# Two experts' rows kept on chip, a diagonal in the first norm, and router logits turned round

## The chip, the cores and the metric

One core of a Trainium2 chip runs the whole kernel. The metric is the device time of one execution in microseconds (us), the median over runs. The engines are TensorE (PE in the profile, with its weight loads as PEld), VectorE (DVE), ScalarE (ACT), GpSimd (POOL) and SyncE (SP), which only issues transfers.

## The reference, cut to what matters

The reference runs four layers over 512 tokens (256 context, 256 latent) of width 1024. Layer i uses attention, Mamba-2, mLSTM or MLA as its mixer and then a hierarchical mixture of 16 experts, of which each token uses two:

```
hx = rmsnorm(xs, norm1_g[i]) * (1.0 + sc1x) + sh1x      # first norm
... mixer ...; xs = xs + g1x * yx
hx = rmsnorm(xs, norm2_g[i]) * (1.0 + sc2x) + sh2x
lg = hx @ w_rg + b_rg                                   # 4 group logits
le = (hx @ w_re + b_re).reshape(4, 4)                   # 16 expert logits
# top group, top two of its experts, softmax weights w
out = sum over e of w[e] * ((silu(hx @ w_gate[e]) * (hx @ w_up[e])) @ w_down[e])
xs = xs + g2x * out
```

The context stream is treated alike with its own shifts, scales and gates. The output is `rmsnorm(xs)` of the latent tokens.

## The kernel before, in words

The residual stream stays on chip as four tiles `X[t]` of 128 tokens by 1024. Instructions are traced in program order and then put into each engine's queue by a scheduler that simulates the engines with a cost model, so an edit can move neighbours that it doesn't touch; `issue_after` pins a block behind one instruction. Weights stream through a ring of on-chip slots (`w`, `wl`) issued from SP.

**First norm** (`norm1_tiles`, four token tiles per layer). ACT squares the tile with a row sum (L289), DVE makes the variance (L291), POOL the power (L293, `rstd`), ACT scales the tile by it into `xn` (L316), TensorE transposes `xn` in eight blocks (L321) into two PSUM tiles `tr`, and ACT (first half, L327) and DVE (second half, L329) evict with scale and shift into `hf`, which is split into `hhi` and `hlo`.

**Router** (`route`, four tiles in layers 0 to 2, two in layer 3). The tile is transposed in eight blocks (L478), ACT copies them into `hT` (L480), and eight fp32 products with `hT` as the loaded weights and the 68 padded router columns `wr` as the moving side make the logits, tokens on partitions, in the PSUM tile `pr` (L482). DVE scales and shifts them (L489). A later chain of small DVE and TensorE steps makes the lists of tokens by expert.

**Experts** (`experts`, layers 0 to 2). Expert e gathers its up to 128 rows from DRAM, multiplies by gate and up (`gate_up`), and one expert later by down (`down`). The scaled rows `y` (L795, L796) are written to a DRAM table `yd` (`keep`, L800) for experts 0 to 14, from POOL, the last one from ACT. Expert 15's rows stay on chip as a pair `yh`, `yl` (L831, L832), with a selector `selT` that maps its slots to tokens.

**Combine** (`combine`, run inside the next layer's first norm). Eight indirect gathers on POOL (L931, two per token tile in the order `go`, the second of a tile adding onto the first) fetch each token's two rows from `yd`; rows of expert 15 point at a row of zeros. For each tile and half, TensorE adds `selT` times `yh` and `yl` (L942, L943) and the gathered rows through an identity product (L946) in one PSUM tile, DVE multiplies by the gate (L947) and adds to `X[t]` (L952, in part POOL, L950). The first L942 of a tile is pinned behind the last expert's last product (`end`).

L248 is a POOL memset of the next layer's modulation step, L225 the product of that step (weights `cs` of 32 columns in four column groups).

Of the kernel before, what the change touches and what calls it, by code (L numbers as in the profile page):

```python
# [7 lines left out]
F32 = mybir.dt.float32  # L8
# [15 lines left out]
class Trunk:  # L24
# [8 lines left out]
    def setup(self):  # L33
# [32 lines left out]
        self.ge = mask(OP.is_ge, F32, "mge")  # L66
        self.le = mask(OP.is_le, F32, "mle")
        self.gtb = mask(OP.is_gt, BF, "mgtb")
        self.onesb = self.const.tile([128, 128], BF, name="onesb")
        nc.vector.memset(self.onesb, 1.0)  # L70
        self.onesf = self.const.tile([128, 128], F32, name="onesf")
# [232 lines left out]
    def norm1_tiles(self, pool, hpool):  # L304
        nc = self.nc
        self.hhi, self.hlo = ([hpool.tile([128, 4, 512], F32R, name=f"h{n}{q}") for q in range(2)] for n in ("hi", "lo"))
        norms, trs = [], [None] * self.o["tl"]
        for t in range(4):
            s = t // 2
            if self.pending:  # L310
                with self.tc.issue_after(norms[-self.o["lag"]].ins) if len(norms) >= self.o["lag"] else ExitStack():
                    self.pending[0](t, trs[-self.o["tl"]])
            xn = pool.tile([128, D], F32, name="xn", bufs=2)
            r = self.rstd(self.X[t], xn)
            norms.append(self.last_var)
            nc.scalar.activation(xn, self.X[t], AF.Copy, scale=r)  # L316
            for h in range(2):
                ps = self.tr()
                for j in range(4):
                    c = (4 * h + j) * 128  # L320
                    tr = nc.tensor.transpose(ps[:, j * 128:(j + 1) * 128], xn[:, c:c + 128], self.ident)  # L321
                hf = pool.tile([128, 4, 128], F32, name="hf", bufs=2)
                for j in range(4):
                    a, b = self.A1[:, s, 4 * h + j:4 * h + j + 1], self.B1[:, s, 4 * h + j:4 * h + j + 1]
                    src = ps[:, j * 128:(j + 1) * 128]
# [4 lines left out]
                hi, lo = self.hhi[h][:, :, t * 128:(t + 1) * 128], self.hlo[h][:, :, t * 128:(t + 1) * 128]  # L330
# [4 lines left out]
                (nc.gpsimd if h < self.o["n1p"] else nc.vector).tensor_sub(lo, hf, hi)  # L335
            trs.append(tr)

    def h(self, j, c0=0, c1=512):
# [75 lines left out]
    def shift_logits(self, i):  # L414

        nc = self.nc

        ps = self.P.tile([128, 512], F32, name="wm", bufs=1)
        for j in range(8):
            nc.tensor.matmul(ps[:32, 0:2], self.wr[:, j, :32], self.shift[:, :, j], start=(j == 0), stop=(j == 7))  # L420
        v = self.const.tile([32, 2], F32, name="bcol")
        nc.vector.tensor_copy(v, ps[:32, 0:2])

        self.bw = self.const.tile([128, 2, 20], F32, name="bw")
        for s in range(2):
            r = ps[:, 64 + 32 * s:96 + 32 * s]
            nc.tensor.matmul(r, v[:, s:s + 1].to_broadcast([32, 128]), self.ident[:32, :32], start=True, stop=True)
            nc.vector.tensor_add(self.bw[:, s], r[:, :20], self.rb[:, i, :])

    def route(self, pool, small, i, tiles, C, dense=False):  # L430
# [10 lines left out]
        lt = le.rearrange("p (t g) k -> p t (g k)", t=T)  # L441
        half = lambda v, h: v.rearrange("p (k h j) -> p h k j", h=2, j=4)[:, h]
        hT, h2s = [], []
        pr = self.core()
        for ti, t in enumerate(tiles):
            s = t // 2
            x = self.X[t]
# [27 lines left out]
            for h in range(2):  # L475
                ps = self.tr()
                for j in range(4):
                    nc.tensor.transpose(ps[:, j * 128:(j + 1) * 128], h2[:, 4 * h + j::8], self.ident)  # L478
                v = ps.rearrange("p (j k) -> p j k", j=4)
                nc.scalar.activation(hT[ti][:, 4 * h:4 * h + 4, :], v, AF.Copy)  # L480
            for j in range(8):
                nc.tensor.matmul(pr[:, ti * 68:(ti + 1) * 68], hT[ti][:, j, :], wr[:, j, :], start=(j == 0), stop=(j == 7))  # L482
            r = None if dense else rows()
            for v, c in ((G, slice(0, 4)), (lt, slice(4, 20))):
                pv = pr[:, ti * 68:ti * 68 + 20][:, c]
                if dense:
                    nc.vector.tensor_add(v[:, ti], pv, bias[:, c])
                else:
                    nc.vector.scalar_tensor_tensor(v[:, ti], pv, r, self.bw[:, s, c], op0=OP.mult, op1=OP.add)  # L489

        def ranks(v, m, nm):

# [47 lines left out]
            nc.vector.tensor_add(self.comb, a12[:, :, 0, :], a12[:, :, 1, :])  # L540
            return

        pp = self.core()
# [74 lines left out]
    def slots_of(self, S, a12, pk, ps, T, oh, weights, count):  # L618
# [7 lines left out]
        nc.vector.tensor_scalar(rw, rw, 128.0 * 15, None, op0=OP.min)  # L626
# [5 lines left out]
        self.last = self.const.tile([128, 4], F32, name="last")  # L632
        t2 = S("t2", [T, 2])
        nc.vector.scalar_tensor_tensor(t2, ps.rearrange("p (t k) -> p t k", k=2), 1.0, a12[:, :, :, 15], op0=OP.add, op1=OP.mult)
# [94 lines left out]
    def experts(self, pool, i, tiles, yd, release):  # L729
# [3 lines left out]
        for x in xgs:  # L733
            nc.gpsimd.memset(x, 0.0)

        nc.gpsimd.dma_start(yd[15 * self.C:, :], xgs[-1][0:1, :])

        def chunk(v):

# [59 lines left out]
        def keep(e, y, eng):  # L799
            return eng.dma_start(yd[e * 128:(e + 1) * 128, :], y)  # L800
# [16 lines left out]
        sel = xgs[0][:, :512].rearrange("p (t k) -> p t k", t=4)  # L817
        pt = self.tr()
        for t in range(4):
            nc.vector.tensor_scalar(sel[:, t], self.slot, self.last[:, t:t + 1], None, op0=OP.is_equal)  # L820
            nc.tensor.transpose(pt[:, t * 128:(t + 1) * 128], sel[:, t], self.ident)
        sT = po.tile([128, 4, 128], F32R, name="selT")
        nc.scalar.activation(sT, pt.rearrange("p (t k) -> p t k", t=4), AF.Copy)
        sw = self.sw[:, 15:16]
# [4 lines left out]
        yh, yl = (po.tile([128, 2, 512], F32R, name="y" + k) for k in "hl")  # L829
        for nb in range(2):  # L830
            nc.scalar.activation(yh[:, nb], py[nb], AF.Copy, scale=sw)  # L831
            nc.vector.scalar_tensor_tensor(yl[:, nb], py[nb], sw, yh[:, nb], op0=OP.mult, op1=OP.subtract)  # L832
        return po, sT, yh, yl

    def experts_select(self, pool, i, tiles):

# [77 lines left out]
            late = s, *now  # L914
        down(7, *late)

    def combine(self, pool, sT, yh, yl, yd, tiles):

        nc = self.nc
        g2 = self.mod_rows(pool, "g2", 2, 1)  # L920
# [15 lines left out]
        def add(t, after=None):  # L936
            x, y, c = self.X[t], ys[t], self.o["cadd"][t]
            for h in range(2):
                k = slice(512 * h, 512 * h + 512)
                ps = self.core() if h in self.o["cc"] else self.acc()  # L940
                with self.tc.issue_after((after or end).ins):
                    nc.tensor.matmul(ps, sT[:, t], yh[:, h], start=True, stop=False)  # L942
                nc.tensor.matmul(ps, sT[:, t], yl[:, h], start=False, stop=False)  # L943
# [1002 lines left out]
    def layers(self, dense=False):  # L1946
# [3 lines left out]
        for i in range(first, 4):  # L1950
# [3 lines left out]
            with self.pool("layer") as self.lay:  # L1954
# [23 lines left out]
                self.wr = route.tile([128, 8, 68], F32, name="wr")  # L1978
# [11 lines left out]
            else:  # L1990
                with self.pool("moe_ring") as L:
# [3 lines left out]
                    listing.close()  # L1995
                    with self.pool("moe_experts") as pool:
                        if i < 3:
                            yd = self.DR.tile([15 * C + 1, D], F32, name=f"yd{i}")
                            last = ExitStack()

                            def release():
# [65 lines left out]
```

## Time and profile before

| what | value |
|---|---|
| time of three runs (median, lowest to highest) | 2086.03 us, 2084.34 to 2087.01 us |
| profiled execution: time, span | 2090.72 us, 2088.8 us |
| mean granted TensorE clock | 0.955 |
| PE, DVE, ACT, POOL busy | 91%, 66%, 50%, 26% of the span |

The span runs from the first to the last instruction; the profiled execution's time holds 1.9 us around it. Matmuls are pipelined and their ends are modelled, so 91% busy is not 91% of what TensorE can do; a time between two starts says more than one duration. Where the chain of waits shows the engine idle is where an edit can give time.

### The profile page before, as it was taken

Reading aid. Unit: us, or ns where it says so; the run is one execution under the profiler, and the core shown is the slowest. Engines: PE = TensorE matmul, PEld = TensorE weight load, DVE = VectorE, ACT = ScalarE, POOL = GpSimd, SP = SyncE. Lnnn points to the kernel's source line nnn. Section 1 sums busy time; section 2 is a strip of 40 time slices with the busy share of each in tenths; the row PEclk is TensorE's granted clock in tenths of the full one; section 3 lists DMA queues with packets and bytes.
Section 4 is the critical chain, followed back from the end, with each engine's and each line's share of the span. In section 5 each row is a group of like instructions: output and inputs, shape, how many; then the busy total and the mean of one; then the engine's idle time right before and its main releaser. Section 6 shows DMA issues by size and latency. Waiting matters only on the chain. (4 is left out here: it accounts for less than half of the span.)

```text
span 2088.8 us, 30243 instructions
## 1 busy us (share of the span) xinstructions
PE 1899.8 (91%) x10820; PEld 1408.4 (67%) x10820; DVE 1387.5 (66%) x2715; ACT 1036.7 (50%) x2144; POOL 537.3 (26%) x528
## 2 busy tenths in 40 slices
PE   5989989997999999998799789997979988998996
PEld 2965677775777777777677467885867755657442
DVE  3668557885697787777788662239578866486443
ACT  4447526774664545432577442245447755454121
POOL 2012232113464646444221310004231122001000
PEclk9999999998999999999899889998989999999998
DMA  9444758976485456547698547543669966708792
GB/s 349 157 152 160 260 173 305 397 280 174 153 261 184 147 186 178 177 147 276 244 393 328 171 146 239 212 153 109 236 206 388 395 199 222 286 11 286 266 366 93
DMA packets 173344, 473.27 MB, mean 227 GB/s; under 512 B 27817, under 2 KB 75041, under 8 KB 152704
## 3 DMA queue, kind: packets, MB, share of 16 engines
q1 hardware_dynamic: 148912, 401.98, 53.7%
q0 software_dynamic: 23568, 67.43, 9.9%
q8 instruction: 88, 1.44, 0.3%
q10 hardware_dynamic: 704, 1.82, 0.2%
q14 instruction: 72, 0.59, 0.1%
HBM read 452.41 MB, written 31.34 MB: 232 GB/s over the span
## 5 line engine op out<-in xcount | busy, mean ns | idle before, releaser
L743 DVE TENSOR_TENSOR elo<-wl,ehi 128x1024 fp32r<-128x1024 f32 x156 | 187.0, 1220 | 23.7 <-ACT ehi L742 22.8
L742 ACT ACTIVATE ehi<-wl 128x1024 fp32r<-128x1024 f32 x156 | 161.3, 1055 | 56.3 <-PE acc L203 32.2
L225 PE MATMUL wm<-w,cs 128*32 128x512 f32 x768 | 125.6, 645 | 21.6 <-DMA w<-in_w_mod_dram 21.4
L748 POOL DMA_INDIRECT xg<-hd,gi x48 | 64.4, 1341 | 288.7 <-PE tr L761 229.6
L1275 POOL TENSOR_TENSOR wcl<-w,wch 128x512 fp32r<-128x512 f32 x76 | 115.0, 1525 | 71.1 <-ACT wch L1274 62.1
L201 PE MATMUL acc<-hhi,wch 128*128 128x512 f32 (+1 forms) x336 | 132.0, 393 | 0.5 <-ACT wch L1274 0.5
L203 PE MATMUL acc<-split_hi,hlo 128*128 128x256 f32 x464 | 131.3, 285 | 0.1
L201 PE MATMUL acc<-split_hi,hhi 128*128 128x256 f32 x464 | 131.2, 287 | 0.0
L202 PE MATMUL acc<-split_lo,hhi 128*128 128x256 f32 x464 | 130.7, 284 | 0.0
L203 PE MATMUL acc<-hhi,wcl 128*128 128x512 f32 (+1 forms) x336 | 129.7, 387 | 0.0
L202 PE MATMUL acc<-hlo,wch 128*128 128x512 f32 (+1 forms) x336 | 129.1, 384 | 0.0
L201 PE MATMUL acc<-ehi,xTh 128*128 128x512 f32 x288 | 124.3, 431 | 3.5 <-ACT xTh L764 3.5
L202 PE MATMUL acc<-elo,xTh 128*128 128x512 f32 x288 | 118.5, 411 | 2.5 <-DVE elo L743 2.5
L203 PE MATMUL acc<-ehi,xTl 128*128 128x512 f32 x288 | 116.4, 404 | 0.0
L743 DVE TENSOR_TENSOR elo<-w,ehi 128x1024 fp32r<-128x1024 f32 x84 | 100.9, 1219 | 13.3 <-ACT ehi L742 13.3
L742 ACT ACTIVATE ehi<-w 128x1024 fp32r<-128x1024 f32 x84 | 87.0, 1052 | 27.5 <-PE acc L203 15.9
L1353 ACT ACTIVATE A<-A,lnb 128x128 f32<-128x128 f32 x256 | 78.9, 390 | 39.9 <-POOL A L1348 39.9
L201 PEld LDWEIGHTS acc<-split_hi,hhi 128*128 128x128 f32 x464 | 88.0, 191 | 11.1 <-issue 5.2
L196 DVE TENSOR_TENSOR split_lo<-w,split_hi 128x1024 fp32r<-128x1024 f32 x33 | 40.2, 1224 | 78.5 <-ACT split_hi L195 78.3
L378 POOL TENSOR_TENSOR x<-x,restmp 128x256 f32<-128x256 f32 (+1 forms) x46 | 50.2, 1091 | 157.9 <-DVE restmp L374 143.7
L203 PEld LDWEIGHTS acc<-split_hi,hlo 128*128 128x128 f32 x464 | 88.6, 191 | 2.7 <-DVE hhi L334 1.7
L202 PEld LDWEIGHTS acc<-split_lo,hhi 128*128 128x128 f32 x464 | 88.6, 191 | 0.7 <-issue 0.7
(621 smaller groups left out, 5432.8 us busy)
## 6 DMA issues: line engine op xcount, KB each, us to landing
w<-in_w_mod_dram SPq DMA_DIRECT2D x96, 1024.0 KB
wl<-in_moe_w_down_dram SPq DMA_DIRECT2D x47, 1024.0 KB
wl<-in_moe_w_gate_dram SPq DMA_DIRECT2D x82, 512.0 KB
wl<-in_moe_w_up_dram SPq DMA_DIRECT2D x82, 512.0 KB
w<-in_moe_w_gate_dram SPq DMA_DIRECT2D x46, 512.0 KB
w<-in_moe_w_up_dram SPq DMA_DIRECT2D x46, 512.0 KB
yd<-y POOLq DMA_DIRECT2D x42, 512.0 KB, 6.8
w<-in_ssm_w_in_dram SPq DMA_DIRECT2D x40, 512.0 KB
```

Source lines behind the costliest of these rows:

```text
L196: self.nc.vector.tensor_sub(lo, w, hi)
L201: mm(ps, a[0], b[0], start=start, stop=False)
L202: mm(ps, a[0], b[1], start=False, stop=False)
L203: self.last_mm = mm(ps, a[1], b[0], start=False, stop=stop)
L225: nc.tensor.matmul(st["ps"][32 * g:32 * g + 32, :], self.cs[:, j, :], w[:, 512 * g:512 * g + 512], start=(j == 0), stop=(j == 7))
L378: (nc.vector if last else nc.gpsimd).tensor_add(x, x, tmp)
L742: nc.scalar.activation(hi, v, AF.Copy)
L743: nc.vector.tensor_sub(lo, v, hi)
L748: nc.gpsimd.indirect_dma_start(out=xgs[e % len(xgs)], out_offset=None, in_=self.hd, in_offset=bass.IndirectOffsetOnAxis(ap=self.gi[:, e:e ...
L1275: (eng or self.nc.gpsimd).tensor_sub(lo, v, hi)
L1353: nc.scalar.activation(M[d][:, h, c], M[d][:, h, c], AF.Exp, bias=self.lb[:, c, k:k + 1])
```

## The change

- **Experts.** The rows of expert 14 stay on chip as those of expert 15 do: `yd` holds 14 experts and the zero row, there are two selectors and two pairs `yh`, `yl`, and `combine` adds four products per tile and half before the gathered rows, where there were two. The last write to `yd` is expert 13's, issued from ACT.
- **First norm.** The scaled copy `xn` is gone. DVE makes `dg`, the identity with its rows scaled by `rstd`, and TensorE multiplies `X[t]` blocks (as weights) by `dg`, a plain fp32 product where there was a transpose. In layers 1 to 3 (where `pending` is set) ACT evicts six of a tile's eight blocks, where it evicted four.
- **Router.** `wr` has 32 columns and is now the loaded side; `hT` moves. Product j writes the 32 partitions of column group j mod 4, so four partial sums stand in `part`. ACT copies them into `gl`, and one product with `fold` (four stacked 32 by 32 identities) sums them and turns them back, into the PSUM tile `pp`, which is now taken at the start of `route`.

```diff
+        self.fold = self.const.tile([128, 32], F32, name="fold")
+        nc.vector.tensor_add(self.fold, iv[:, 0], iv[:, 1])
+        for g in (2, 3):
+            nc.vector.tensor_add(self.fold, self.fold, iv[:, g])
...
-            r = self.rstd(self.X[t], xn)
-            nc.scalar.activation(xn, self.X[t], AF.Copy, scale=r)
+            r = self.rstd(self.X[t], pool.tile([128, D], BF, name="sq", bufs=2))
+            dg = pool.tile([128, 128], F32, name="dg", bufs=2)
+            nc.vector.tensor_scalar(dg, self.ident, r, None, op0=OP.mult)
...
-                    tr = nc.tensor.transpose(ps[:, j * 128:(j + 1) * 128], xn[:, c:c + 128], self.ident)
+                    tr = nc.tensor.matmul(ps[:, j * 128:(j + 1) * 128], self.X[t][:, c:c + 128], dg, start=True, stop=True)
...
-                    if h == 0:
+                    if h == 0 or (self.pending and j < 2):
...
-        pr = self.core()
+        pr, pp = self.core(), self.core()
...
+            part = pr[:, ti * 128:(ti + 1) * 128]
             for j in range(8):
-                nc.tensor.matmul(pr[:, ti * 68:(ti + 1) * 68], hT[ti][:, j, :], wr[:, j, :], start=(j == 0), stop=(j == 7))
+                g = 32 * (j % 4)
+                nc.tensor.matmul(part[g:g + 32], wr[:, j, :], hT[ti][:, j, :], start=(j < 4), stop=(j > 3))
+            gl = small.tile([128, 128], F32, name="gl", bufs=2)
+            nc.scalar.activation(gl, part, AF.Copy)
+            pv = pp[:, 128 + ti * 32:160 + ti * 32]
+            nc.tensor.matmul(pv, gl, self.fold, start=True, stop=True)
...
+        keep(13, y, nc.scalar)
         po = release()
-        keep(13, y, nc.gpsimd)
-        y = rows(14, down(*late))
-        keep(14, y, nc.scalar)
-        py = down(*gate_up(15, x))
+        for u in range(2):
+            sel = xgs[u][:, :512].rearrange("p (t k) -> p t k", t=4)
+            ...
+            py = down(*(gate_up(15, x) if u else late))
+            yh, yl = (po.tile([128, 2, 512], F32R, name=f"y{k}{u}") for k in "hl")
...
+                    for u, (sT, yh, yl) in enumerate(kept):
+                        nc.tensor.matmul(ps, sT[:, t], yh[:, h], start=(u == 0), stop=False)
+                        nc.tensor.matmul(ps, sT[:, t], yl[:, h], start=False, stop=False)
```

The row limit of the gathers, the table's size and the slot table `last` (one more small DVE step) follow.

## Rows read from the trace of the kernel before

**Rows 1.** Instructions of L946: until what TensorE sat idle (us, times).

```profile
  DMA w<-yd,ri: 51.5, 13
```

**Rows 2.** Timeline, layer 0 to 1: start, length, engine, line [idle before <- releaser].

```profile
465.00 0.69 ACT L796 ACTIVATE y<-core,slotw 128x512 f32<-128x512 f32 x1 [0.28 <-PE core L203]
...
472.59 0.35 ACTq L800 DMA_DIRECT2D yd<-y  x1
...
474.19 0.52 POOL L248 MEMSET mod<- 64x512 f32 x1 [7.67 <-DVE elo L743]
...
476.23 1.09 POOL L931 DMA_INDIRECT w<-yd,ri  x1 [1.52 <-DMA yd<-y]
...
479.83 0.39 PE L203 MATMUL core<-ehi,actTl 128*128 128x512 f32 x1
...
481.66 0.62 PE L943 MATMUL acc<-yl,selT 128*128 128x512 f32 x2
...
490.07 2.08 PE L946 MATMUL acc<-w,ident 128*128 128x512 f32 x2 [7.10 <-DMA w<-yd,ri]
```

**Rows 3.** Timeline, layer 1 to 2.

```profile
1157.59 0.69 ACT L796 ACTIVATE y<-core,slotw 128x512 f32<-128x512 f32 x1 [0.27 <-PE core L203]
...
1168.69 1.09 POOL L931 DMA_INDIRECT w<-yd,ri  x1 [1.37 <-DMA yd<-y]
...
1174.00 0.40 PE L203 MATMUL core<-ehi,actTl 128*128 128x512 f32 x1
...
1182.30 2.08 PE L946 MATMUL acc<-w,ident 128*128 128x512 f32 x2 [5.15 <-DMA w<-yd,ri]
```

**Rows 4.** Timeline, layer 2 to 3.

```profile
1694.44 0.69 ACT L796 ACTIVATE y<-core,slotw 128x512 f32<-128x512 f32 x1 [0.27 <-PE core L203]
...
1705.45 1.09 POOL L931 DMA_INDIRECT w<-yd,ri  x1 [7.54 <-DMA yd<-y]
...
1709.28 0.39 PE L203 MATMUL core<-ehi,actTl 128*128 128x512 f32 x1
...
1719.38 2.08 PE L946 MATMUL acc<-w,ident 128*128 128x512 f32 x2 [6.96 <-DMA w<-yd,ri]
...
1729.67 2.07 PE L946 MATMUL acc<-w,ident 128*128 128x512 f32 x2 [2.65 <-DMA w<-yd,ri]
```

**Rows 5.** Stretches: length, PE, PEld, DVE, ACT, POOL busy, clock, DMA, GB/s.

```profile
483.00:490.00 7.00, 0.00 (x0) 0.00 (x0) 1.13 (x2) 0.02 (x1) 5.37 (x4) 0.80 1.04 231
490.00:495.00 5.00, 4.93 (x7) 2.18 (x8) 1.76 (x3) 0.00 (x0) 0.00 (x0) 0.59 1.06 210
...
505.00:511.00 6.00, 3.12 (x16) 2.54 (x15) 4.73 (x14) 6.00 (x12) 1.48 (x2) 0.50 1.04 311
```

**Rows 6.** The experts' own gathers (min/median/max ns), instructions of L748.

```profile
L748 POOL DMA_INDIRECT xg<-hd,gi x48: 984/1412/1902, 308.7 to 1647.9; - x48
```

**Rows 7.** Groups by line and shape: busy us, mean ns.

```profile
L743 DVE TENSOR_TENSOR elo<-wl,ehi 128x1024 fp32r<-128x1024 f32 x156 | 187.0, 1220 | 23.7 <-ACT ehi L742 22.8
...
L316 ACT ACTIVATE xn<-x,rstd 128x1024 f32<-128x1024 f32 x16 | 18.3, 1150 | 11.5 <-POOL rstd L293 11.5
```

**Rows 8.** Timeline, first norm of layer 1 and Mamba-2 core: runs of like instructions.

```profile
511.48 1.50 ACT L327 ACTIVATE hf<-tr,B,A 128x128 f32<-128x128 f32 x4
...
515.66 1.03 PE L321 MATMUL tr<-ident,xn 128*128 128x128 f32 x8
...
605.24 0.83 PE L1376 MATMUL tr<-CT,st 128*128 128x128 f32 x6
```

**Rows 9.** Timeline, routers of layers 0 and 3, and one modulation step.

```profile
40.72 1.07 PE L225 MATMUL wm<-w,cs 128*32 128x512 f32 x8
...
289.32 0.67 PE L420 MATMUL wm<-shift,wr 128*32 128x2 f32 x16
...
297.72 1.90 PE L482 MATMUL core<-wr,h2T 128*128 128x68 f32 x16
...
1924.44 3.66 PE L482 MATMUL core<-wr,h2T 128*128 128x68 f32 x16 [2.70 <-DVE le L489]
```

More of the change, by code (lines that the diff above doesn't have):

```diff
@@ L68, in setup @@
         self.gtb = mask(OP.is_gt, BF, "mgtb")
+        self.fold = self.const.tile([128, 32], F32, name="fold")
+        iv = self.ident.rearrange("p (g c) -> p g c", g=4)
+        nc.vector.tensor_add(self.fold, iv[:, 0], iv[:, 1])
+        for g in (2, 3):
+            nc.vector.tensor_add(self.fold, self.fold, iv[:, g])
         self.onesb = self.const.tile([128, 128], BF, name="onesb")
@@ L312, in norm1_tiles @@
                     self.pending[0](t, trs[-self.o["tl"]])
-            xn = pool.tile([128, D], F32, name="xn", bufs=2)
-            r = self.rstd(self.X[t], xn)
+            r = self.rstd(self.X[t], pool.tile([128, D], BF, name="sq", bufs=2))
             norms.append(self.last_var)
-            nc.scalar.activation(xn, self.X[t], AF.Copy, scale=r)
+            dg = pool.tile([128, 128], F32, name="dg", bufs=2)
+            nc.vector.tensor_scalar(dg, self.ident, r, None, op0=OP.mult)
+            tok = slice(t * 128, (t + 1) * 128)
             for h in range(2):
@@ L329, in norm1_tiles @@
                         nc.vector.tensor_scalar(hf[:, j, :], src, a, b, op0=OP.mult, op1=OP.add)
-                hi, lo = self.hhi[h][:, :, t * 128:(t + 1) * 128], self.hlo[h][:, :, t * 128:(t + 1) * 128]
+                hi, lo = self.hhi[h][:, :, tok], self.hlo[h][:, :, tok]
                 if h:
@@ L334, in norm1_tiles @@
                     nc.vector.tensor_copy(hi, hf)
-                (nc.gpsimd if h < self.o["n1p"] else nc.vector).tensor_sub(lo, hf, hi)
+                nc.vector.tensor_sub(lo, hf, hi)
             trs.append(tr)
@@ L419, in shift_logits @@
         for j in range(8):
-            nc.tensor.matmul(ps[:32, 0:2], self.wr[:, j, :32], self.shift[:, :, j], start=(j == 0), stop=(j == 7))
+            nc.tensor.matmul(ps[:32, 0:2], self.wr[:, j, :], self.shift[:, :, j], start=(j == 0), stop=(j == 7))
         v = self.const.tile([32, 2], F32, name="bcol")
@@ L625, in slots_of @@
         nc.vector.tensor_add(rw, rw, ps)
-        nc.vector.tensor_scalar(rw, rw, 128.0 * 15, None, op0=OP.min)
+        nc.vector.tensor_scalar(rw, rw, 128.0 * 14, None, op0=OP.min)
         self.ri = self.const.tile([128, 8], I32, name="ri")[:, :T * 2]
@@ L630, in slots_of @@
         count()
-        self.last = self.const.tile([128, 4], F32, name="last")
-        t2 = S("t2", [T, 2])
-        nc.vector.scalar_tensor_tensor(t2, ps.rearrange("p (t k) -> p t k", k=2), 1.0, a12[:, :, :, 15], op0=OP.add, op1=OP.mult)
+        self.last = self.const.tile([128, 2, 4], F32, name="last")
+        t2 = S("t2", [2, T, 2])
+        for u in range(2):
+            nc.vector.scalar_tensor_tensor(t2[:, u], ps.rearrange("p (t k) -> p t k", k=2), 1.0, a12[:, :, :, 14 + u],
+                                           op0=OP.add, op1=OP.mult)
         nc.vector.tensor_reduce(self.last, t2, axis=AX.X, op=OP.add)
@@ L734, in experts @@
             nc.gpsimd.memset(x, 0.0)
-        nc.gpsimd.dma_start(yd[15 * self.C:, :], xgs[-1][0:1, :])
+        nc.gpsimd.dma_start(yd[14 * self.C:, :], xgs[-1][0:1, :])
         def chunk(v):
@@ L814, in experts @@
             x, late = nx, now
+        keep(13, y, nc.scalar)
         po = release()
[L817 to L824, printed above, removed]
-        keep(13, y, nc.gpsimd)
-        y = rows(14, down(*late))
-        keep(14, y, nc.scalar)
-        py = down(*gate_up(15, x))
[L829 to L833, printed above, removed]
+        kept = []
+        for u in range(2):
+            sel = xgs[u][:, :512].rearrange("p (t k) -> p t k", t=4)
+            pt = self.tr()
+            for t in range(4):
+                nc.vector.tensor_scalar(sel[:, t], self.slot, self.last[:, u, t:t + 1], None, op0=OP.is_equal)
+                nc.tensor.transpose(pt[:, t * 128:(t + 1) * 128], sel[:, t], self.ident)
+            sT = po.tile([128, 4, 128], F32R, name=f"selT{u}")
+            nc.scalar.activation(sT, pt.rearrange("p (t k) -> p t k", t=4), AF.Copy)
+            py = down(*(gate_up(15, x) if u else late))
+            sw = self.sw[:, 14 + u:15 + u]
+            yh, yl = (po.tile([128, 2, 512], F32R, name=f"y{k}{u}") for k in "hl")
+            for nb in range(2):
+                nc.scalar.activation(yh[:, nb], py[nb], AF.Copy, scale=sw)
+                nc.vector.scalar_tensor_tensor(yl[:, nb], py[nb], sw, yh[:, nb], op0=OP.mult, op1=OP.subtract)
+            kept.append((sT, yh, yl))
+        return po, kept
     def experts_select(self, pool, i, tiles):
@@ L915, in experts_select, with combine @@
         down(7, *late)
-    def combine(self, pool, sT, yh, yl, yd, tiles):
+    def combine(self, pool, kept, yd, tiles):
         nc = self.nc
@@ L1977, in layers @@
                 self.A2 = self.mod_rows(route, "A2", 2, 0)
-                self.wr = route.tile([128, 8, 68], F32, name="wr")
+                self.wr = route.tile([128, 8, 32], F32, name="wr")
                 self.router_weights(self.wr, i)
@@ L1997, in layers @@
                         if i < 3:
-                            yd = self.DR.tile([15 * C + 1, D], F32, name=f"yd{i}")
+                            yd = self.DR.tile([14 * C + 1, D], F32, name=f"yd{i}")
                             last = ExitStack()
```

8 lines of the change are left out of this document (2 added, 6 removed).

## Prediction

> **What bounds the kernel now.** I read the page first: TensorE is busy nearly everywhere, so time can come only from stretches in which it stands idle or runs at its lower clock. The view of one line's waits then tells where: before the identity products of the combine TensorE sat idle 51.5 us in all until gathered rows landed [rows 1] (a wait of the weight load and of its product are counted apart, so the wall time is about half of that). The timeline of the three layer changes shows how it comes about. In the first, expert 14's write to `yd` is issued at 472.59, the first gather can start at 476.23, when that write has landed, and the first product on gathered rows at 490.07, after 7.10 us of idle TensorE [rows 2]. The second and third look alike, with 5.15 and 6.96 us, and the third waits 2.65 us more on a later tile [rows 3, 4]. The view of stretches adds the clock: 0.80 granted in the idle stretch, 0.59 in the 5 us behind it, 0.50 in the norm [rows 5]. So the end is set there by write, gather, product, and then by a chain through DVE and ACT, not by TensorE's work.
>
> **The change, part by part.** The sum is made against the profiled execution, 2090.72 us; the median of three runs is 2086.03, 0.22% less, and the forecast is scaled to it.
>
> *A. The gathers start earlier.* Expert 14's write is gone; the last one is expert 13's. Its rows are ready at 465.00 + 0.69 = 465.69 [rows 2]. From issue on ACT to the first gather took 476.23 - 472.59 = 3.64 us [rows 2]; I take the same, so the first gather goes at 469.3, 6.9 us earlier. The write moves from POOL's queue to ACT's; there it holds the next weight conversion by about the 0.35 us that the issue took [rows 2], while the same issue for expert 14 falls away. The gathers keep their place in POOL's queue, and SP's next weight loads, which wait for the two ring slots that the gathered rows hold, move up with the additions that free them. From first gather to first product took 490.07 - 476.23 = 13.84 us [rows 2], so the rows are there at 483.2. Then TensorE itself is later: its last expert product starts at 479.83, and before the gathered rows come the selector products of the five pairs of tile and half for which PSUM has room, now 20 passes instead of 10, at 0.62 - 0.39 = 0.23 us each [rows 2]: 479.83 + 0.23 + 20 x 0.23 = 484.7. So the first identity product starts at 484.7, not 490.07: -5.4. In the second change 1158.28 + 3.64 + 13.84 = 1175.8 against 1174.00 + 21 x 0.23 = 1178.8, so -3.5 [rows 3]; in the third 1712.6 against 1709.28 + 4.83 = 1714.1, so -5.3 [rows 4]. Together -14.2. What is late next is TensorE, then DVE's gate products and additions, on which the other six selector passes hide (1.4 us a change, +4.1 in all if that cover is gone). Bounds: nothing if the gather is held by something else, -20.7 if the extra passes are covered too.
>
> Gathers now run under expert 15's weight splits on DVE, of 1.22 us each [rows 7], where they ran under little. The nearest rows are the experts' own gathers, which run under such splits: 1.41 us in the median, 0.98 at the least [rows 6], so 0.4 us more for each of the four gathers ahead of the first tile, 1.6 us; in the first change that makes 484.8 against TensorE's 484.7, and nothing in the sum. The Trainium skill, page "SBUF — State Buffer", section "Who interferes with whom", says that a DVE instruction with two SBUF inputs and a GpSimd instruction that reads SBUF shut each other out for a whole instruction; were each gather held by one whole split, the time would be that of the third rival, and the trace so far shows a third of that.
>
> *B. No cold start behind the wait.* In the 5 us behind the idle stretch the clock was 0.59 [rows 5]; without the stretch the same work takes 5 x 0.59 = 2.95 us at the full level, -2.0 for each of three changes, and the third saves its later 2.65 as well [rows 4], since its gathers are through before the modulation weights' loads set in. -8.7; bounds 0 (the clock stays low, DVE sets the pace) and -14 (the norm behind it warm too).
>
> *C. First norm.* Out of each tile's chain goes the scaled copy, 1.15 us [rows 7]. In comes `dg`, which no row shows: between nothing and one 128 by 128 eviction, 1.50 / 4 = 0.375 us [rows 8]; an eighth of a split of 1024 elements would be 0.15 [rows 7], so I take 0.25. A transposed block costs one pass; eight take 1.03 us. The plain fp32 product of the same shape in Mamba-2 is recorded as two passes, and six of those take 0.83, so a pass costs (1.03 - 0.83) / 2 = 0.10 in either form [rows 8]. Four blocks ahead of the first eviction then cost 0.40 more at the full level. Net -0.50 a tile; ACT's load per tile falls by 1.15 - 2 x 0.375 = 0.40, which bounds what a stage in which ACT is busy 6.00 of 6.00 us [rows 5] can give: about -1.5 in each of layers 1 to 3, -0.5 in layer 0, where the norm waits for modulation weights. -5.0. Bounds: at the half level, with all eight extra passes on the path, -1.15 + 0.25 + 8 x 0.20 = +0.7 a tile, +11; or the whole copy gained, -14.
>
> *D. Router.* The 16 passes of a tile's logits take 1.90 us [rows 9]. Turned round they load 32 columns and write four column groups. Bounds: 1.90 if nothing overlaps, and 0.67, which 16 passes with 32 loaded columns and two moving ones take [rows 9]. Nearest is the modulation product, eight passes of 512 columns in four groups in 1.07 us [rows 9], four times as much streaming a pass, so I take 0.8. New are the copy `gl` on ACT (0.375 as above) and two passes of `fold` (0.20): in the last tile they eat the gain; in the three tiles ahead 0.90 each is left, of which DVE's and ACT's own steps leave half: -1.3 in each of layers 0 to 2. In layer 3 the second tile's logits waited 2.70 us for DVE to read the first's out of the same PSUM tile [rows 9]; ACT now empties it: -2. Sum -5.9. The added wait is `fold`'s for ACT; behind it on TensorE stand the next tile's transposes. If they stand there each time, 14 tiles x 0.6 = +8.4; at best -14.
>
> *E. Small change.* Four more selector transposes per layer, 4 x 0.11, lie in the TensorE-bound expert loop: +1.3. Expert 14's split rows take DVE and ACT one step more than its plain rows; they lie under TensorE's products of expert 15. The zero-row write, `last` and `fold`'s set-up lie beside the lists and the first weight loads.
>
> Sum: -14.2 - 8.7 - 5.0 - 5.9 + 1.3 = -32.5: 2058.2 for the profiled execution, 2086.03 x (1 - 32.5 / 2090.72) = 2053.6 for the median.
>
> **The rivals.**
> 1. *The memset stays in front.* L248 waited on POOL until 474.19 for the experts' space and took 0.52 [rows 2]. If the scheduler leaves it ahead of the gathers, they start at 474.7 in the first change, 1.5 us earlier, and I take the same for the second; the third keeps its -5.3. A becomes -8.3, B loses 4.0: -22.6, 2063.5. For it: it stood there. Against: it came in while the gathers waited.
> 2. *The gain is eaten by the new TensorE waits.* C and D at their bad bounds: -14.2 - 8.7 + 11 + 8.4 + 1.3 = -2.2, 2083.8, no change. For it: 0.50 in the norm [rows 5]. Against: the clock fell behind idle TensorE, and the norm will have twice the passes; the transposes ahead of `fold` belong to other tiles.
> 3. *Gathers starve under the splits.* Each of the four gathers held by one split, 4.9 us: 488.1, 1180.7 and 1717.5, A = -2.0 - 1.6 - 1.9 = -5.5, and B's idle is back by half, -4.4: -19.5, 2066.6.
> 4. *Slower: the plain products cost four passes.* If a block against `dg` took four passes of 0.20, at the half level and on the norm's path, a tile would pay 8 x (0.80 - 0.20) = 4.8 less the 0.9 that copy and `dg` differ by, 16 tiles +62 in C's place: +34.5, 2120.5. It decides from 27.5 / 16 = 1.7 us a tile. Against it: two passes, each of 0.10 at the full level [rows 8]. The Trainium skill, "TensorE: Matmul & The Clock Gate", section "Terms", calls the transpose mode four times faster for fp32; row L1376 shows twice.
>
> **How the numbers follow.** Forecast 0.60; rival 1 0.18; rival 3 0.08; rival 2 0.08; rival 4 0.04; 0.02 for other ways of being slower. The range takes the forecast's own spread (B at -13, C and D doubled: about 2038) up to rival 1 with C and D at nothing (2074.4): 2038 to 2075. About 0.2%, 4 us, is what a measurement of this kernel can tell from no change; faster (the forecast, rivals 1 and 3) 0.86, same (rival 2) 0.08, slower 0.06.
>
> **What would show it.** In the changed trace the first gather goes 3 to 4 us after expert 13's rows, ahead of L248; L946's wait for gathered rows falls from 51.5 to under 10; the clock behind the last expert stays near 1.00. In the norm a tile has 16 passes at 0.10 and no L316. The 16 logit passes of a tile take under 1 us, and the fold stands clear of ACT's long steps. Wrong it would be if the gathers start no earlier than L248 ends, if the norm runs at 0.50 with TensorE waited for, or if TensorE idles ahead of `fold` in each tile.

## The result and the profile after

The changed kernel takes 2064.12 us (median of four runs) against 2086.52 us of the kernel before: ratio 0.9884, 95% interval 0.9869 to 0.9898. The forecast was 2053.6 us in a range of 2038 to 2075. The profiled execution went from 2090.72 to 2062.44 us, by 28.3 us. Of this, 22.4 us is the medians' difference; the profiled execution of before lay 4.2 us above its median and that of after 1.7 us below. So stretches read from the two traces sum to some 6 us too much. The two medians alone give a ratio of 0.9893; where variants are compared below by their ratios, each is taken against the kernel before in its own round, and the medians can give a difference that is up to 4 us another.

First, what TensorE waited for ahead of the identity products (L963 of the changed kernel). The row answers to [rows 1], where it stood at 51.5 us:

```profile
  DMA w<-yd,ri: 5.8, 6
```

The timeline of the first layer change answers to [rows 2]:

```profile
466.59 0.69 ACT L811 ACTIVATE y<-core,slotw 128x512 f32<-128x512 f32 x1 [0.33 <-PE core L209]
...
467.31 0.35 ACTq L815 DMA_DIRECT2D yd<-y  x1
...
470.38 1.23 DVE L758 TENSOR_TENSOR elo<-wl,ehi 128x1024 fp32r<-128x1024 f32 x1 [0.56 <-ACT ehi L757]
...
470.97 1.59 POOL L947 DMA_INDIRECT w<-yd,ri  x1 [9.49 <-DMA yd<-y]
...
472.67 2.36 DVE L758 TENSOR_TENSOR elo<-wl,ehi 128x1024 fp32r<-128x1024 f32 x2 [1.06 <-ACT ehi L757]
...
472.86 1.93 POOL L947 DMA_INDIRECT w<-yd,ri  x1 [0.30 <-issue]
...
475.10 1.00 POOL L947 DMA_INDIRECT w<-yd,ri  x1 [0.30 <-issue]
...
477.41 0.54 POOL L254 MEMSET mod<- 64x512 f32 x1
...
483.07 0.40 PE L209 MATMUL core<-ehi,actTl 128*128 128x512 f32 x1
...
487.84 1.02 PE L963 MATMUL acc<-w,ident 128*128 128x512 f32 x2
...
488.71 1.02 PE L963 MATMUL core<-w,ident 128*128 128x512 f32 x2
```

The first gather goes 470.97 - 467.28 = 3.69 us after expert 13's rows are ready, the memset stands behind four gathers, and the first identity product follows the last expert product after 4.77 us of selector products, without a wait and at the full level (1.02 us for two, 2.08 before). It is 2.2 us earlier than before, not 5.4: expert 13's rows are 1.6 us later than before, and the last expert product another 1.6 us.

The other two changes can be read from expert 13's rows to the first identity product, before [rows 3, 4] and after:

```profile
1145.02 0.69 ACT L811 ACTIVATE y<-core,slotw 128x512 f32<-128x512 f32 x1 [0.33 <-PE core L209]
...
1164.38 1.13 PE L963 MATMUL acc<-w,ident 128*128 128x512 f32 x2 [1.76 <-DMA w<-yd,ri]
...
1675.11 0.69 ACT L811 ACTIVATE y<-core,slotw 128x512 f32<-128x512 f32 x1 [0.33 <-PE core L209]
...
1696.43 1.02 PE L963 MATMUL acc<-w,ident 128*128 128x512 f32 x2
```

That way takes 20.56, 18.67 and 20.63 us where it took 24.38, 24.02 and 24.25: -3.8, -5.3 and -3.6, together -12.8 us. In the second change TensorE still waits 1.76 us for rows.

The view of stretches, to be held against [rows 5] (clock 0.59 behind the idle stretch, 0.50 in the norm):

```profile
487.80:492.80 5.00, 5.00 (x14) 2.27 (x13) 3.69 (x5) 1.05 (x2) 0.40 (x1) 1.00 1.01 200
502.70:508.70 6.00, 5.91 (x37) 5.94 (x38) 3.15 (x9) 4.37 (x12) 0.55 (x1) 0.72 1.10 378
```

In the second change the whole norm is warm as well. Its 17 us, of before (from L321's first row on, at 1193), then of after (from L329's, at 1177):

```profile
1193.00:1210.00 17.00, 6.24 (x33) 4.56 (x32) 15.62 (x35) 15.54 (x32) 1.55 (x3) 0.62 0.32 111
```

```profile
1177.00:1194.00 17.00, 14.47 (x116) 12.48 (x115) 12.67 (x34) 12.88 (x31) 2.73 (x7) 1.00 0.63 219
```

The norm and the router by line, over the whole run (busy us, mean ns). Of before: L321 21.0 us in 128 passes, L482 30.6 us in 224.

```profile
L329 PE MATMUL tr<-dg,x 128*128 128x128 f32 x256 | 36.1, 292 | 5.1 <-ACT hf L335 3.0 <-DVE var L297 1.7 <-DVE hf L337 0.3
...
L493 PE MATMUL core<-h2T,wr 128*32 128x128 f32 x224 | 11.5, 293 | 1.6 <-ACT h2T L489 1.3
L497 PE MATMUL core<-fold,gl 128*128 128x32 f32 x28 | 5.6, 283 | 4.9 <-ACT gl L495 4.4 <-DVE le L503 0.5
```

TensorE has 15.1 us more to do in the norm and 13.5 us less in the router. Steps of their timelines, against [rows 8, 9]:

```profile
297.62 0.64 PE L493 MATMUL core<-h2T,wr 128*32 128x128 f32 x16
...
298.33 0.28 ACT L495 ACTIVATE gl<-core 128x128 f32<-128x128 f32 x1
...
299.64 0.41 PE L497 MATMUL core<-fold,gl 128*128 128x32 f32 x2
...
497.60 1.95 PE L329 MATMUL tr<-dg,x 128*128 128x128 f32 x16
...
497.94 0.28 DVE L323 TENSOR_SCALAR dg<-ident,rstd 128x128 f32<-128x128 f32 x1
```

**A ledger by stretch.** Like instructions that occur equally often in two traces are matched in order; the median difference of their starts is how far the later kernel is ahead at that place, and a row is how much that changed over a stretch (us, negative is gained, each against the profiled execution of before). "Change 0 to 1" reaches from expert 13's rows to about 60 us behind the combine. The columns other than the first are experiments of the next section. The profiled executions lie off their medians by different amounts: in the order of the columns -1.7, 0.0, 0.0, 2.3, 1.1, 6.0 and 5.6 us, so that a difference between two columns is off by as much.

```
stretch                    whole  experts  norm  router  no norm  no router  late write
layer 0 up to its router     3.2     1.0    2.8     1.4      0.5        3.3         2.8
router 0                    -2.3     0.0    0.0    -2.3     -2.3        0.0        -2.3
change 0 to 1               -6.1    -6.4   -3.4     1.3     -5.4       -7.5        -1.8
rest of Mamba-2, router 1   -8.6     0.7    3.3    -9.7     -2.1       -2.2        -7.4
change 1 to 2              -10.3   -10.6    0.7     1.6    -11.3      -10.0        -5.3
rest of mLSTM                4.4     2.3    3.9     0.4     -1.9        7.7         3.9
router 2                    -1.5     0.6    0.3    -2.0     -2.2       -0.1        -2.0
change 2 to 3               -6.9    -8.4    1.7     0.9     -3.9       -2.9         1.3
rest of MLA                  1.3     7.4    1.0     7.1      0.1        0.5         0.7
router 3                    -2.0     0.1    0.3    -2.0     -2.0       -0.1        -2.0
lists, experts, last layer   1.3     1.1   -0.8    -1.1      1.1        1.2         1.7
sum                        -27.5   -12.3    9.9    -4.4    -29.4      -10.1       -10.4
```

In the whole, the layer changes give 23.3 us, near the 22.9 of A and B; the norms of layers 1 to 3, for which C had 4.5 more, lie in the same rows. But mixers that the change doesn't touch move by up to 9 us either way, and layer 0 loses 3.2. The experiments ask what each part is worth and where these come from.

### The profile page after: what moved, and what is told of

It is laid out like the page before. It is cut to its first block, busy times and chain, and to the rows that moved or that the text cites. A ratio compares the mean times of both kernels' runs of the same rounds, so it can differ in the third digit from the quotient of the medians.

```text
span 2060.3 us, 30756 instructions
## 1 busy us (share of the span) xinstructions
PE 1899.6 (92%) x11036; PEld 1411.8 (69%) x11036; DVE 1394.9 (68%) x2728; ACT 1036.1 (50%) x2172; POOL 536.4 (26%) x525
```

## The experiments

**The three parts alone**, each the lines of the change that belong to it. Of the experts' part:

```diff
+        keep(13, y, nc.scalar)
...
+        for u in range(2):
...
+                    for u, (sT, yh, yl) in enumerate(kept):
```

> The kernel before with the experts' part of the change alone (rows of experts 14 and 15 on chip; first norm and router as before). By the sum it carries A, B and E: -14.2 - 8.7 + 1.3 = -21.6 us, a ratio of 0.9897. The trace of the changed kernel gives for the same part -7.0, -2.0 and -11.7 at the three layer changes and +1.4 in lists and experts: -19.3, 0.9908. Rival: the earlier gathers pay only with the new norm, because behind the combine the old norm's chain through ACT would be late next; then about half, -10 us, 0.995.

Measured: 2077.27 us, ratio 0.9962 (0.9947 to 0.9977). At the three layer changes the trace gives 25.4 us, so the rival falls there, though its number (0.995, half the gain for want of the new norm) is near: 7.4 us go again in MLA, which no expectation had.

```diff
-            nc.scalar.activation(xn, self.X[t], AF.Copy, scale=r)
...
+            nc.vector.tensor_scalar(dg, self.ident, r, None, op0=OP.mult)
```

> The kernel before with the first norm's part alone. By the sum C = -5.0 us, ratio 0.9976. From the changed kernel's trace (+3.2 in layer 0's norm and mixer, -7.1, -2.5 and +4.5 in the three others) -1.9 us, 0.9991, with layer 0 later by some 3 us. Rival: the bad bound of C, all extra passes at the half clock on the path, +11 us, 1.0053.

Measured: 2100.27 us, ratio 1.0075 (1.0057 to 1.0093). The number is beyond the rival's, but its mechanism is not what the trace shows: where the new norms stand, the ledger has +2.8 in layer 0 and -3.4, +0.7 and +1.7 at the three changes, together +1.8. The rest is in mixers and in an odd place, the unchanged router of layer 1. Its timeline and stretch in this kernel (L484 is the router's product):

```profile
976.25 0.40 PE L429 MATMUL wm<-ident,bcol 32*128 32x32 f32 x2 [3.25 <-DVE var L291]
...
983.55 3.52 PE L484 MATMUL core<-wr,h2T 128*128 128x68 f32 x16
...
992.64 3.65 PE L484 MATMUL core<-wr,h2T 128*128 128x68 f32 x16 [0.55 <-DVE le L491]
```

```profile
980.00:990.00 10.00, 10.00 (x49) 9.60 (x48) 5.78 (x12) 2.98 (x5) 3.67 (x5) 0.50 0.98 386
990.00:998.00 8.00, 5.75 (x26) 5.41 (x26) 2.03 (x10) 0.00 (x0) 0.00 (x0) 0.50 0.18 71
```

The router ran at the lower level, 3.5 us for what takes 1.90 [rows 9], and the kernel fell back by 7.7 us between the end of Mamba-2 and the lists. Of this, 5.0 are in the products' own time in this router (13.9 us busy, 8.9 before). Early in it TensorE waited 3.25 us; in the kernel before, 1.35 at the same step, and there the later products ran at the full level:

```profile
981.74 0.40 PE L427 MATMUL wm<-ident,bcol 32*128 32x32 f32 x2 [1.35 <-DVE bcol L422]
...
989.62 1.90 PE L482 MATMUL core<-wr,h2T 128*128 128x68 f32 x16
```

That the longer wait is why the clock fell and stayed low is not shown: no run takes the wait away.

```diff
-                nc.tensor.matmul(pr[:, ti * 68:(ti + 1) * 68], hT[ti][:, j, :], wr[:, j, :], start=(j == 0), stop=(j == 7))
...
+                nc.tensor.matmul(part[g:g + 32], wr[:, j, :], hT[ti][:, j, :], start=(j < 4), stop=(j > 3))
```

> The kernel before with the router's part alone. By the sum D = -5.9 us, ratio 0.9972. The changed kernel's trace gives -2.3, -1.9, -1.9 and -2.2 in the four routers, -8.3 us, 0.9960. Rival: the fold's wait for ACT holds TensorE each time, +8.4 us, 1.0040.

Measured: 2083.99 us, ratio 0.9993 (0.9979 to 1.0007). Routers 0, 2 and 3 gain 2.0 to 2.3 us each, as in the whole, and MLA gives 7.1 back. The product of the three ratios is 1.003; the whole is 0.9884. The parts don't add up.

**The whole less one part** (diffs against the changed kernel). First without the norm's lines:

```diff
+            xn = pool.tile([128, D], F32, name="xn", bufs=2)
...
+            nc.scalar.activation(xn, self.X[t], AF.Copy, scale=r)
...
-            dg = pool.tile([128, 128], F32, name="dg", bufs=2)
```

> The change without its first-norm part. If C is worth its -5.0 us in the whole, this is slower than the changed kernel by that much: 0.9908. If the parts' own times added up (-8.0 us for the experts, -1.5 for the router), 0.9955. If the norm's part is worth nothing and what the experts' part alone lost came from products split apart elsewhere (22 pieces of layer 3's modulation products there, 19 here), the gains at the layer changes (-25) and in the routers (-8) stand: about 0.985 to 0.987.

Measured: 2059.65 us, ratio 0.9869 (0.9847 to 0.9890): no slower than the changed kernel. The norm's part gives nothing in the whole; a gain of 5 us (0.9908 here) is outside the interval.

Then without the router's:

```diff
-        pr, pp = self.core(), self.core()
+        pr = self.core()
...
+                nc.tensor.matmul(pr[:, ti * 68:(ti + 1) * 68], hT[ti][:, j, :], wr[:, j, :], start=(j == 0), stop=(j == 7))
```

> The change without its router part. If D is worth -5.9 us in the whole, 0.9912; by the trace's -8.3 us, 0.9924. If the parts' own times added up (-8.0 and +13.6 us), 1.003.

Measured: 2073.50 us, ratio 0.9933 (0.9908 to 0.9958). The router's part is worth (0.9933 - 0.9884) x 2086 = 10 us in the whole, with an uncertainty of about 6; the forecast was 5.9. The two profiled executions differ by 17.1 us, since that of this kernel lay 6.0 above its median.

**Layer 0's norm as before**, all else as in the changed kernel:

```diff
+            if self.pending:
+                nc.vector.tensor_scalar(dg, self.ident, r, None, op0=OP.mult)
+            else:
+                nc.scalar.activation(dg, self.X[t], AF.Copy, scale=r)
```

> The changed kernel, but in layer 0 alone the first norm scales a copy on ACT and transposes it, as before. If the diagonal form costs layer 0 its lateness of 3.2 us at the router, the time falls from the changed kernel's ratio of 0.9884 to about 0.987, and the profile's first router product comes some 3 us earlier. Rival: the lateness comes from later transfers of the modulation weights; then it stays at 0.988 and the router is as late.

Measured: 2054.44 us, ratio 0.9858 (0.9838 to 0.9878). The router of layer 0 starts 3.1 us earlier than in the changed kernel, as expected if the diagonal form costs it. The time fell by 9.7 us by the medians and 5.4 by the ratios, with intervals that just overlap; most of what is beyond the 3.1 is in mLSTM (7.7 us by the method of the ledger). The changed kernel's last modulation step ahead of that norm with the norm's first row, and this kernel's:

```profile
32.86 1.93 PE L231 MATMUL wm<-w,cs 128*32 128x512 f32 x8 [1.54 <-DMA w<-in_w_mod_dram]
...
36.52 3.16 PE L329 MATMUL tr<-dg,x 128*128 128x128 f32 x16
```

```profile
31.97 1.91 PE L231 MATMUL wm<-w,cs 128*32 128x512 f32 x8 [0.55 <-DMA w<-in_w_mod_dram]
...
35.20 1.36 PE L338 MATMUL tr<-ident,xn 128*128 128x128 f32 x8
```

Sixteen passes came at the lower level (0.20 each); eight took 1.36. Of the 3.1 us, 1.3 are there before this row starts, as the modulation weights ahead of it land 0.9 us later; the rest comes with and behind the longer row. So the expectation's rival has a part in it too: the norm's edit moves those weights as well, and why is not shown.

**The write of expert 13 held back** until expert 14's rows are scaled:

```diff
-        keep(13, y, nc.scalar)
...
+            if not u:
+                with self.tc.issue_after(act.ins):
+                    keep(13, y, nc.scalar)
```

> The changed kernel, but expert 13's write to the table is queued behind the scaling of expert 14's rows, so that the gathers start about as late as before the change, with all else the same. If A and B are what the experts' part is worth, their 22.9 us come back: ratio 0.9994, first gathers some 5 to 7 us later and TensorE waiting for gathered rows again. Rival: the gain comes from the smaller table and the fewer gathered rows; then it stays near 0.988.

Measured: 2073.57 us, ratio 0.9940 (0.9921 to 0.9960), 11.7 us slower than the changed kernel, with an uncertainty of about 5; 22.9 were expected. The first gather goes at 477.08 instead of 470.97 and TensorE waits for rows again (before L964 of this kernel, in us and times):

```profile
  DMA w<-yd,ri: 27.6, 10
```

The cold start is back with the wait (2.08 us for two products, 1.02 in the changed kernel):

```profile
491.06 2.08 PE L964 MATMUL acc<-w,ident 128*128 128x512 f32 x2 [2.99 <-DMA w<-yd,ri]
```

The ledger loses 4.3, 5.0 and 8.2 us at the three changes, 17.5 together, but its two executions differ by 16.7 us where the runs differ by 11.7. So the start of the gathers is worth about half of the 22.9 by the runs and three quarters by the traces; that the smaller table gave all of it falls. A part of the rest may stay because 20 selector passes now run in the wait, where 10 ran before (10 x 0.23 us in each change); this, and a share of the smaller table, no run separates.

**Half the selector products** (the low parts of the two experts' rows are left out of the sum):

```diff
-                        nc.tensor.matmul(ps, sT[:, t], yl[:, h], start=False, stop=False)
```

> The changed kernel without the products with the low parts yl of the two experts' rows (that part of the sum is left out): 10 selector passes instead of 20 ahead of the first gathered rows. If A ends at TensorE because of those passes, 2.3 us less at each layer change and up to 1.4 more behind, -7 to -11 us: 0.985 to 0.983. Rival: gathers or DVE hold the combine; then it stays at 0.988 and TensorE waits for rows instead.

Measured: 2055.18 us, ratio 0.9854 (0.9836 to 0.9872), 6 us less than the changed kernel by the midpoints, with intervals that just overlap. The first two changes gain 2.4 and 2.1 us, the third loses 3.3, which leaves 1.2 of what was to be 7 to 11; 7.6 us of the trace's gain are in mLSTM, as with layer 0's norm as before. The wait for rows (L962 here) is back at

```profile
  DMA w<-yd,ri: 22.0, 17
```

In the first two changes TensorE's passes were the limit, with 2.3 us expected of each, and the gathers stand close behind them: fewer passes turn into waiting.

**One column group** for the logits instead of four:

```diff
-            part = pr[:, ti * 128:(ti + 1) * 128]
+            part = pr[:32, ti * 128:(ti + 1) * 128]
...
-                g = 32 * (j % 4)
-                nc.tensor.matmul(part[g:g + 32], wr[:, j, :], hT[ti][:, j, :], start=(j < 4), stop=(j > 3))
+                nc.tensor.matmul(part, wr[:, j, :], hT[ti][:, j, :], start=(j == 0), stop=(j == 7))
...
```

> The changed kernel, but the router's eight products of a tile sum in one column group of 32 partitions, and the fold is a product with a 32 by 32 identity. If D's gain comes from four column groups running side by side, the 16 passes of a tile go from 0.64 to some 1.8 us, and the time rises by 4 us (the last tile of each router) to 9 us (the others in part): 0.9905 to 0.993. Rival: the gain comes from the shorter weight loads or the later chain; then it stays at 0.988.

Measured: 2080.51 us, ratio 0.9974 (0.9961 to 0.9987), 19 us slower than the changed kernel, twice the most that was expected. The passes of one tile:

```profile
298.69 1.94 PE L492 MATMUL core<-h2T,wr 128*32 128x128 f32 x16
```

1.94 against 0.64 us: the overlap of the four groups is the whole gain. Without it router 0 is 2.5 us slower than before the change, and by the method of the ledger each router of layers 0 to 2 loses 4.5 to 5.1 us against the changed kernel, where 1 to 2.3 were expected. The Trainium skill, "TensorEngine Tiling (Array Packing)", section "Performance Considerations", names this swap of the loaded and the moving side with fourfold column tiling for 32 columns, and its section "Theoretical Speedup" gives up to four times for such a dimension; the rows here show 1.94 / 0.64 = 3.0.

**Modulation products kept together.** Both the experts' part and the router's part alone lost 7 us in MLA, where nothing waited more. The trace shows the modulation products (L225, four column groups for each weight tile) cut into smaller pieces by the scheduler's new order. The experts' part alone, timeline of MLA:

```profile
1778.41 1.08 PE L1853 MATMUL tr<-ident,qrow 128*96 128x128 f32 x8
1779.42 1.05 PE L225 MATMUL wm<-w,cs 128*32 128x512 f32 x2
1780.40 0.39 PE L201 MATMUL acc<-upkv_hi,ckvh 128*128 128x256 f32 x1
...
1781.30 1.04 PE L225 MATMUL wm<-w,cs 128*32 128x512 f32 x2
1782.28 0.39 PE L201 MATMUL acc<-upkv_hi,ckvh 128*128 128x256 f32 x1
```

A piece of two passes holds TensorE for 0.98 us, while all eight together take 1.07 [rows 9]. The edit puts layer 3's pieces at high priority:

```diff
+            with self.tc.high_priority() if i == 3 else ExitStack():
+                for g in range(4):
...
```

> The experts' part alone, with layer 3's modulation products at high priority, so that the four column groups of a step stay together in TensorE's queue (15 pieces where there were 22). If the split groups are what gave 7 us back in layer 3's mixer, the time falls by 6 us below that of the experts' part alone: ratio 0.993, and the 64 passes take 9.6 us instead of 15.8. Rival: the split only fills time in which TensorE would wait for something else; then it stays at 0.996.

Measured: 2064.23 us, ratio 0.9897 (0.9876 to 0.9917), 13.5 us less than the experts' part alone (9.7 between the profiled executions, of which 8.2 in MLA by the method of the ledger). The same 64 passes of MLA, first in the experts' part alone, then here:

```profile
L225 PE MATMUL wm<-w,cs 128*32 128x512 f32 x64 | 15.8, 605 | 0.0
```

```profile
L226 PE MATMUL wm<-w,cs 128*32 128x512 f32 x64 | 8.5, 605 | 0.0
```

So the cut pieces cost the 7 us that MLA gave back, and that is shown. That the router's part alone lost its 7.1 us in the same way is read from its trace alone (15.8 us there too).

**The same in layers 1 to 3**, on the two fastest kernels so far:

```diff
+            with self.tc.high_priority() if self.layer > 0 else ExitStack():
```

> The changed kernel with layer 0's first norm as before and the modulation products of layers 1 to 3 at high priority, so that a step's four column groups stay together (24 pieces of TensorE's queue in layer 1 where there were 30). A piece of two passes takes the 1.05 us that one of eight takes, so six pieces fewer are worth about 5 us if TensorE is the limit there: 0.9858 becomes about 0.983. Rival: these products fill time in which TensorE waits anyway, then it stays at 0.986.

Measured: 2056.11 us, ratio 0.9860 (0.9842 to 0.9877): nothing gained over 0.9858. The modulation products hold TensorE for less time in the whole run (111.3 us, 125.3 without the priority), and the time doesn't follow. The rival's number came, but not for its reason. In layer 1 the 192 passes hold TensorE 26.0 us (36.0 without the priority), and by the method of the ledger this kernel is 8.4 us ahead of the one without it when layer 1's experts end. All of it is lost again between there and the end of mLSTM's first projections. In these TensorE now waits for a modulation weight, and the products behind it run at the lower level at first:

```profile
1245.35 1.94 PE L232 MATMUL wm<-w,cs 128*32 128x512 f32 x8 [4.88 <-DMA w<-in_w_mod_dram]
```

Without the priority no wait stands there (TensorE is busy for 10.00 of 10.00 us in 1235 to 1245 of that kernel, 5.47 here). So the pieces did hold up layer 1; put first everywhere, they meet a transfer that is not there yet.

> The change without its norm part, with the same high priority: 24 pieces in layer 1 instead of 31 and 15 in layer 3 instead of 19, some 9 us by the same price: 0.9869 becomes about 0.983. Rival: 0.987.

Measured: 2054.32 us, ratio 0.9839 (0.9819 to 0.9859). This is the change without its norm part, and it beats both kernels; that it beats the same kernel without the priority (0.9869) is not settled, since the intervals overlap. It too is 12.0 us ahead of that kernel when layer 1's experts end, and loses that by mLSTM's projections.

## Why the prediction was right, and where not

**A and B, -22.9: right.** The layer changes give 20.6 us without the norm's part, 25.4 with the experts' part alone and 23.3 in the whole, and 11.7 (runs) to 17.5 (traces) of them go when the write is late. The steps hold too: 3.69 us from rows to gather (3.64 taken), 4.77 from last product to first identity product (4.83 taken), -12.8 us from rows to first identity product in the three changes (-14.2 taken), clock 1.00 behind the last expert. By change it was less even: -6.1, -10.3, -6.9 for -7.4, -5.5, -10.0. At the second the bound "norm warm too" came true; the first loses to an expert tail that is 3.2 us later, which no term had (1.6 of it lies in the ledger's rows ahead). A's bound of -20.7 is three times the first change's 6.9; by its own rows it is 6.9 + 6.5 + 6.8 = -20.2.

**C, -5.0: wrong.** The norm's part gives nothing in the whole (0.9869 without it) and costs 15.7 us alone. The failed step is "-0.50 a tile": it charged four of a tile's eight extra passes, at the full level, and took the others as hidden behind ACT's saving. Together they are 15.1 us of TensorE, and in layer 0 they come at 0.20 each, +3 us with the later weights for the -0.5 forecast. At the three changes the part gives 2.7 us in the whole and 1.0 alone, for 4.5. That the part alone came out beyond the bad bound of +11 is not that bound's mechanism: its own places sum to +1.8 there. In the whole, held against the version without it, the ledger has those 2.7 us taken back by 2.7 in layer 0, and the mixers cancel (6.5 better in Mamba-2, 6.3 worse in mLSTM).

**D, -5.9: right mechanism, too small.** A tile's passes take 0.64 us (0.8 taken), `gl` 0.28 (0.375), `fold` 0.41 (0.20). The mis-sized step is "in the last tile they eat the gain": by the prediction's own numbers 1.90 - 0.80 - 0.375 - 0.20 = 0.5 us were left there. A router gives about 2 us, not 1.3. The part is worth 10 us in the whole, with an uncertainty of 6, so that about 8 in the routers is all that the ledger places. Of the added wait, 4.4 us of TensorE stand before the fold in the whole run, not 0.6 in each tile.

**E, +1.3:** the ledger's row says +1.3, but it is a sum of two things. By the ledger's method the changed kernel falls back by 1.3 us in each of the three expert loops, 3.9 in all, and lists and the last layer give the rest back. The experts' part alone falls back by some 0.65 in each, near the 0.44 forecast, and the router's part alone by some 0.85, for which there was no term.

**The rivals.** The memset went behind the gathers (1 falls, though its 2063.5 us is the number nearest to the measured one). The first two gathers were stretched to 1.59 and 1.93 us, the next two not, 1.5 us in all where the sum had 1.6; in the first change TensorE came later than their rows (3 falls). A block against `dg` is two passes, 0.12 us each (4 falls). Rival 2 falls: the norm's part at no gain is not its +11, and the routers gained.

**What the sum left out.** Each part reorders queues far from it: modulation pieces cut in MLA (7 us, shown), a router at the lower clock (7.7 us, read from the trace), Mamba-2 with its router between -9.7 and +3.3, mLSTM between -1.9 and +7.7. A part of Mamba-2's row goes with layer 1's modulation pieces, by the traces alone: its 192 passes hold TensorE 39.0 us before, 36.0 in the whole, 33.5 with the router's part alone, 38.9 with the experts' part alone. In mLSTM the granted clock differs; of the changed kernel and, at the like place, of the one with layer 0's norm as before:

```profile
1420.00:1430.00 10.00, 6.16 (x36) 5.77 (x36) 8.96 (x19) 3.13 (x11) 6.42 (x6) 0.76 0.00 1
```

```profile
1419.00:1429.00 10.00, 8.40 (x63) 6.74 (x65) 10.00 (x30) 6.02 (x21) 5.65 (x5) 1.00 0.10 43
```

Why mLSTM moves stays open. In the whole these rows happened to sum to little: Mamba-2 with its router -8.6, of which the router explains 2, mLSTM +4.4, MLA +1.3, layer 0 +3.2. The sum was -32.5 for -28.3 between the profiled executions. That it missed by only 4.2 us is in part luck: C gave nothing for its -5.0, D gave more than its -5.9, and the rows that no term held came to little. The other 6 us between 2053.6 and 2064.1 are the two profiled executions' distances from their medians, 4.2 and 1.7.

## What to carry to other kernels

When a stage waits for a transfer, move the start of the last write that it depends on and fill the rest with work that is ready; count that filling work as the next limit. In a kernel that one engine nearly fills, price an edit by the busy time that it adds to that engine as well as by the chain that it shortens, and trust neither alone: here +15.1 us of TensorE in the norm cost next to nothing, -13.5 in the router gave about 10, and -14.0 in the modulation products gave nothing in the end. Test the parts of a change by leaving each out of the whole as well as alone, for a scheduler that reorders everything can make the two differ by more than a part is worth.

## What the hardware showed unexpectedly

- An indirect gather that is issued on POOL while DVE splits a weight is held for what is left of the split, not for the whole of it. The first gather goes at 470.97, 0.64 us before the split of 470.38 ends, and takes 1.59 us; the second at 472.86 with about 1.0 us of a split left, and takes 1.93; the next two, under no split, take 1.00. The other two changes show the same (1.75 and 1.92 us, 1.89 and 1.93), and the first two gathers of the late write, under no split, take 1.08 and 1.03.
- A piece of two passes in 32-column groups between products of 128 columns holds TensorE for 0.98 us, nearly as long as eight passes kept together (1.07). The Trainium skill, "TensorEngine Tiling (Array Packing)", section "Tiling Modes", says that a change of tiling mode drains the engine; the rows don't contradict it, but leave it little: an identity product, two passes of as many columns without such a change, takes 488.71 - 487.84 = 0.87 us from start to start. So most of the cost of a cut piece is the lost overlap of the four groups.
- An unchanged router took 7.7 us longer, 5.0 of it in its products, with the clock at a granted 0.50: 16 passes took 3.5 to 3.65 us, where 1.90 is the time at the full level.
- Gathers of the combine landed a median 5.8 us after their issue where it had been 9.7, though two in each change were issued under splits on DVE.
